# A transformer block on one core: the down projection's operands are split five pairs ahead of their products in place of three

## The chip, the cores and the metric

The kernel runs on one core of one Trainium2 chip. The metric is device time in microseconds (us): lower is better. A core has a matrix engine (TensorE, in the profile PE), a vector engine (VectorE, DVE), a scalar engine (ScalarE, ACT), a general engine (GpSimd, POOL) and a queue that only issues transfers (SyncE, SP). Each engine works through its own list of instructions in order; semaphores tie the lists together.

## The reference, cut to what matters

One decoder layer over 1024 tokens of width 1024, in float32: a mixer (pooling and differential attention, merged and projected), then a SwiGLU feed-forward with a hidden width of 2816, each with an RMSNorm before and after and a residual. The change touches only the last line's product and what follows it:

```python
h = h + rms_norm(einsum('bsd,de->bse', m, w_out), mix_post_g)
u = rms_norm(h, ffn_pre_g)
f = silu(einsum('bsd,df->bsf', u, w_ffn_gate)) * einsum('bsd,df->bsf', u, w_ffn_up)
h = h + rms_norm(einsum('bsf,fd->bsd', f, w_ffn_down), ffn_post_g)
```

## The kernel before, in words

**Precision.** Each float32 operand is split into a high part (a cast to the format that TensorE multiplies, `fp32r`) and a low part (the operand less its high part). A product is three matmuls, high x high, high x low and low x high (`triple`, lines 233 to 235). The cast runs on ScalarE (`split`, line 166), the subtraction on VectorE (`sub`, line 89).

**Seven products.** The down projection f x w_ffn_down is cut in four quadrants and done with seven half-size products in place of eight (a Strassen-like scheme). Each product takes one combination S of the hidden activations, kept in DRAM (`fsd`), and one combination T of the weights, summed in place in SBUF (`wsum`, line 149). The hidden width of a half is 1408, 11 slices of 128; so there are 7 x 11 = 77 pairs (product, slice kb). For one pair `operands` (lines 1180 to 1184) makes two tiles, `s_op` and `w_op`, each with a high and a low part of 128 x 512; TensorE then runs four row tiles x three matmuls, 12 in all. `down_block` accumulates them in the PSUM banks Y, X or Z (`Yd`, `Xd`, `Zd` in the profile).

**Buffers.** `s_op`, `w_op` and the broadcast gain `g2post` come from one pool, `b4`, of 14 buffers. `g2post` keeps one to the end. The raw activations are loaded two slices at a time (`load_s`, line 1176) into the pool `wraw`, two buffers; a buffer is loaded again only when both of its slices have been cast and subtracted.

**The order.** The loop walks the 77 pairs. At pair n it issues the load for pair n + DEPTH + 3, makes the operands of pair n + DEPTH, and then writes the products of pair n. Outside of two stretches written out by hand (not here) a scheduler decides the order in which each engine gets its instructions; the source order and the free buffers are what it starts from.

**The end.** The last product (A22, T4) goes to Y. Its first six slices (SPLIT = 6, kb 0 to 5) are done pair by pair over four row tiles; slices 6 to 10 are done row tile by row tile, 15 matmuls each, so that a tile's end can be finished while the next is multiplied. Beside the first six slices the kernel finishes output tiles 0 to 3: sum of squares (ScalarE, line 130), mean (VectorE, line 1219, `fms`), multiply by the gain (GpSimd, line 1212, `c`), reciprocal root (GpSimd, line 1221, `frstd`), the scaled residual sum in two halves (VectorE, line 1234, `hr`), and two stores issued from ScalarE's queue (line 1236). Tiles 4 to 7 follow with stores from SyncE's queue; their residual loads (line 1225, `hr`) take the buffers of tiles 0 to 3 and so wait for those tiles' stores.

Of the kernel before, what the change touches and what calls it, by code (L numbers as in the profile page):

```python
# [41 lines left out]
def block_kernel(ctx, tc, x, w_in, pool_mix, pool_scale, w_branch_a, lam_q1, lam_k1, lam_q2,  # L42
# [1194 lines left out]

    g2post = b4([P, D], F32, "g2post")
    nc.sync.dma_start(g2post, ffn_post_g.partition_broadcast(P))
    kept, loaded, DEPTH, SPLIT = {}, {}, 3, 6  # L1240
    PARTS = [(0, HALF), (HALF, D)]
    LAST_PARTS = [(HALF, D), (0, 256), (256, HALF)]
    PRODUCTS = [("A11", "B11"), ("S1", "T1"), ("S2", "T2"), ("S4", "B22"), ("S3", "T3"), ("A12", "B21"), ("A22", "T4")]
# [89 lines left out]
```

## Time and profile before

| what | value |
|---|---|
| median of 3 runs | 1273.1 us (1270.13, 1273.1, 1273.31) |
| span of the profiled execution | 1265.6 us |
| ScalarE, busy | 582.7 us (46%) |
| VectorE, busy | 838.6 us (66%) |
| mean granted TensorE clock | 0.998 |

The profile is one execution; its page lists its span, from the first to the last instruction, and no device time of its own. The runs' times also hold what lies ahead of and behind the span. In the rows of the views, a line gives start and duration in us, engine, source line, operation, output <- inputs; a bracket at its end gives the idle time of the engine just before it and what ended it. A group of rows gives the count and the mean. A row of a wait view reads: engine, line <- what it waited for: us in total, times, longest. "ACTq" and "SPq" are the transfers that ScalarE's and SyncE's queues issue.

### The profile page before, as it was taken

The numbers are of one execution on the slowest core, as the hardware profiler recorded it, in microseconds if no ns is written. First come the engines' busy times: TensorE is split into PE (matmuls) and PEld (weight loads), VectorE is DVE, ScalarE is ACT, GpSimd is POOL, SyncE is SP. The second block draws the span as 40 slices with busy tenths as digits, with TensorE's granted clock in tenths as the row PEclk, the third lists the DMA queues.
The fourth block names the chain that finished last, engine by engine and source line by source line (L and its number), as shares of the span: only waits on it lengthen the run. The fifth ranks groups of instructions, "written<-read, shape, count | busy, mean of one in ns | idle before, by whom it ended". The sixth has DMA issues, their size and how long they took to land.

```text
span 1265.6 us, 15699 instructions
## 1 busy us (share of the span) xinstructions
PE 1246.5 (98%) x5912; PEld 1039.1 (82%) x5912; DVE 838.6 (66%) x1296; ACT 582.7 (46%) x1042; POOL 142.7 (11%) x128
## 2 busy tenths in 40 slices
PE   8999999999999999999999999999999999999997
PEld 7888888888788887888888888888888888888886
DVE  5985784534578888855697655655656547955666
ACT  7553344434477774444553333333333333554542
POOL 4100000000201100000102111011111011000221
PEclk9999999999999999999999999999999999999999
DMA  7354338323797108533314322323322368733236
GB/s 253 114 189 132 135 128 243 115 85 117 259 250 206 34 18 283 169 115 134 117 45 139 125 100 89 103 100 108 125 99 84 125 215 279 238 95 105 87 96 208
DMA packets 135452, 179.15 MB, mean 142 GB/s; under 512 B 7632, under 2 KB 90320, under 8 KB 132944
## 3 DMA queue, kind: packets, MB, share of 16 engines
q1 hardware_dynamic: 124544, 146.56, 37.0%
q10 hardware_dynamic: 10832, 31.59, 6.5%
q8 instruction: 46, 0.75, 0.3%
q14 instruction: 30, 0.25, 0.1%
HBM read 124.39 MB, written 53.74 MB: 141 GB/s over the span
## 4 chain that ended last, share of the span: by engine, by line
PE 89%; DVE 3%; ACT 2%; DMA 2%; issue 2%; POOL 1%; SPq 0%; POOLq 0%; DVEq 0%; ACTq 0%
PE Y L235 10%; PE Y L234 10%; PE Y L233 10%; PE X L235 5%; PE X L234 5%; PE X L233 5%; PE Z L235 3%; PE Z L234 3%; PE Z L233 3%; PE Yd L234 3%; PE Yd L235 3%; PE Yd L233 3%; PE o L792 2%; PE branch L233 2%; PE branch L235 2%; PE branch L234 2%
## 5 line engine op out<-in xcount | busy, mean ns | idle before, releaser
L162 DVE TENSOR_TENSOR p<-Z,p 128x512 f32<-128x512 f32 x35 | 24.2, 691 | 163.3 <-PE Z L235 160.7
L234 PE MATMUL Y<-A_lo,Wh 128*128 128x512 f32 x296 | 115.5, 390 | 0.3 <-DVE A_lo L89 0.3
L233 PE MATMUL Y<-A_hi,Wh 128*128 128x512 f32 x296 | 115.2, 389 | 0.0
L235 PE MATMUL Y<-A_hi,Wl 128*128 128x512 f32 x296 | 115.2, 389 | 0.0
L233 PE MATMUL Y<-S_hi,Wh 128*128 128x512 f32 x280 | 109.2, 390 | 0.0
L233 PE MATMUL X<-S_hi,Wh 128*128 128x512 f32 x280 | 109.2, 390 | 0.0
L235 PE MATMUL Y<-S_hi,Wl 128*128 128x512 f32 x280 | 109.1, 390 | 0.0
L234 PE MATMUL Y<-S_lo,Wh 128*128 128x512 f32 x280 | 109.1, 390 | 0.0
L235 PE MATMUL X<-S_hi,Wl 128*128 128x512 f32 x280 | 108.9, 389 | 0.0
L234 PE MATMUL X<-S_lo,Wh 128*128 128x512 f32 x280 | 108.9, 389 | 0.0
L202 ACT CAST Wh<-wf_t 128x1024 fp32r<-128x1024 f32 x70 | 72.8, 1053 | 72.1 <-PE X L234 30.6
L202 ACT CAST Wh<-w_raw 128x1024 fp32r<-128x1024 f32 x72 | 60.6, 843 | 66.7 <-PE Z L234 40.0
L89 DVE TENSOR_TENSOR w_op<-wd,w_op 128x512 fp32r<-128x512 f32 x77 | 56.1, 729 | 52.8 <-ACT w_op L166 52.6
L89 DVE TENSOR_TENSOR Wl<-wf_t,Wh 128x1024 fp32r<-128x1024 f32 x70 | 86.6, 1245 | 4.8 <-ACT Wh L202 4.8
L166 ACT CAST w_op<-wd 128x512 fp32r<-128x512 f32 x77 | 47.9, 622 | 78.1 <-PE Yd L235 31.4
L89 DVE TENSOR_TENSOR Wl<-w_raw,Wh 128x1024 fp32r<-128x1024 f32 x72 | 70.4, 977 | 14.5 <-ACT Wh L202 14.5
L233 PE MATMUL Yd<-w_op,s_op 128*128 128x512 f32 x176 | 68.7, 390 | 0.6 <-ACT w_op L166 0.6
L234 PE MATMUL Yd<-w_op,s_op 128*128 128x512 f32 x176 | 68.7, 390 | 0.3 <-DVE w_op L89 0.3
L235 PE MATMUL Yd<-w_op,s_op 128*128 128x512 f32 x176 | 68.3, 389 | 0.0
L162 DVE TENSOR_TENSOR wf_t<-w_raw,wf_t 128x512 f32<-128x512 f32 x70 | 65.7, 938 | 1.1
L234 PEld LDWEIGHTS Y<-A_lo,Wh 128*128 128x128 f32 x296 | 55.6, 188 | 12.1 <-DVE A_lo L89 0.7
L233 PEld LDWEIGHTS Y<-A_hi,Wh 128*128 128x128 f32 x296 | 55.6, 188 | 11.6
(269 smaller groups left out, 3058.7 us busy)
## 6 DMA issues: line engine op xcount, KB each, us to landing
s_raw<-fsd SPq DMA_DIRECT2D x35, 512.0 KB, 3.6
w_raw<-in_w_in_dram SPq DMA_DIRECT2D x32, 512.0 KB, 4.3
w_raw<-in_w_ffn_gate_dram SPq DMA_DIRECT2D x22, 512.0 KB, 3.8
w_raw<-in_w_ffn_up_dram SPq DMA_DIRECT2D x22, 512.0 KB, 3.8
fsd<-fss SPq DMA_DIRECT2D x11, 1024.0 KB, 3.9
wd<-in_w_ffn_down_dram SPq DMA_DIRECT2D x44, 256.0 KB, 5.4
fsd<-F SPq DMA_DIRECT2D x33, 256.0 KB, 2.3
qkd<-qk_st ACTq DMA_DIRECT2D x16, 512.0 KB, 3.8
```

The costliest lines, as they stand in the source:

```text
L89: nc.vector.tensor_tensor(out=o, in0=a, in1=f32(hi), op=ALU.subtract)
L162: nc.vector.tensor_tensor(out=o, in0=a, in1=b, op=op)
L166: nc.scalar.copy(hi, a)
L202: nc.scalar.copy(hi, a)
L233: nc.tensor.matmul(o, ah, bh, start=start, stop=False, skip_group_check=goes_on)
L234: nc.tensor.matmul(o, ah, bl, start=False, stop=False, skip_group_check=goes_on)
L235: nc.tensor.matmul(o, al, bh, start=False, stop=stop, skip_group_check=goes_on)
L792: nc.tensor.matmul(o, ats[b // 4][:, j, b % 4 * P:(b % 4 + 1) * P], V[:, b, :, :], start=b == 0 and j == 0, stop=b == qb and j == 1)
```

## The change

One number: the loop keeps the operands of five pairs ahead of the products in place of three. Because the load distance is DEPTH + 3, loads are written eight pairs ahead in place of six. Pools, buffer counts, products and their order in the source stay as they are.

```diff
-    kept, loaded, DEPTH, SPLIT = {}, {}, 3, 6
+    kept, loaded, DEPTH, SPLIT = {}, {}, 5, 6
```

The lines that use it, unchanged:

```python
for n in range(DEPTH + 3):
    fetch(n)
for n in range(DEPTH):
    ready[n] = operands(*PRODUCTS[stream[n][0]], stream[n][1])
for n, (i, kb) in enumerate(stream):
    fetch(n + DEPTH + 3)
    if n + DEPTH < len(stream):
        j, kj = stream[n + DEPTH]
        ready[n + DEPTH] = operands(*PRODUCTS[j], kj)
```

## The prediction

> **What bounds the kernel now.** I read the page first, for the busy engine. It gives one span, of 1265.6 us; the median of the runs shown is 1273.1 us, so 7.5 us lie around the span. I make the sum against the span and carry the same difference over to the median.
>
> ```profile
> span 1265.6 us, 15699 instructions
> PE 1246.5 (98%) x5912; PEld 1039.1 (82%) x5912; DVE 838.6 (66%) x1296; ACT 582.7 (46%) x1042; POOL 142.7 (11%) x128
> ```
>
> TensorE is busy 98% of the span. Converting operands earlier can save only what TensorE loses waiting for operands of the down projection. So the second view is who TensorE waited for, over the whole span; only these two of its rows name the down projection (Yd, fed by w_op):
>
> ```profile
> PE Yd L233 <- ACT w_op L166: 0.6, 1, 0.6
> PE Yd L234 <- DVE w_op L89: 0.3, 1, 0.3
> ```
>
> One wait each, 0.9 us together. The third view, TensorE's instructions in order of time, shows where they are:
>
> ```profile
> 1227.48 0.39 PE L233 MATMUL Yd<-w_op,s_op 128*128 128x512 f32 x1
> ...
> 1243.80 0.39 PE L233 MATMUL Yd<-w_op,s_op 128*128 128x512 f32 x1
> ...
> 1245.84 0.39 PE L233 MATMUL Yd<-w_op,s_op 128*128 128x512 f32 x1
> 1246.23 0.50 PE L234 MATMUL Yd<-w_op,s_op 128*128 128x512 f32 x1
> 1246.56 0.40 PE L235 MATMUL Yd<-w_op,s_op 128*128 128x512 f32 x1
> 1247.58 0.50 PE L233 MATMUL Yd<-w_op,s_op 128*128 128x512 f32 x1 [0.62 <-ACT w_op L166]
> 1248.39 0.50 PE L234 MATMUL Yd<-w_op,s_op 128*128 128x512 f32 x1 [0.31 <-DVE w_op L89]
> ...
> 1248.96 0.39 PE L233 MATMUL Yd<-w_op,s_op 128*128 128x512 f32 x1
> ...
> 1258.96 0.39 PE L235 MATMUL Yd<-w_op,s_op 128*128 128x512 f32 x1
> ```
>
> The last product has pairs 0 to 10 (kb). Pairs 0 to 5 take 72 matmuls from 1227.48 to 1243.80, so a matmul starts every 0.2267 us. From 1243.80 the block's first row tile takes pairs 6 to 10, three matmuls each; 1245.84 is pair 9, 1247.58 is pair 10. From 1245.84 to 1248.96 are six steps, 1.36 us at that pace; they took 3.12. **The whole loss in this product is 1.76 us**, for pair 9's low part and both parts of pair 10. After 1248.96 all is steady.
>
> What made pair 10 late is in the chain that ended last, and in the queues of ScalarE and SyncE:
>
> ```profile
> 1241.31 5.06 DMA s_raw<-fsd
> 1233.76 4.55 ACTq L1236 DMA_DIRECT2D out_dram<-hr  x4
> 1238.35 0.62 ACT L166 CAST s_op<-s_raw 128x512 fp32r<-128x512 f32 x1 [6.68 <-DVE hr L1234]
> 1240.05 1.00 ACTq L1236 DMA_DIRECT2D out_dram<-hr  x2
> 1246.39 0.62 ACT L166 CAST s_op<-s_raw 128x512 fp32r<-128x512 f32 x1 [1.19 <-DMA s_raw<-fsd]
> 1246.92 0.61 ACT L166 CAST w_op<-wd 128x512 fp32r<-128x512 f32 x1
> 1237.50 0.33 SPq L1225 DMA_DIRECT2D hr<-h1d  x1
> 1241.31 0.33 SPq L1176 DMA_DIRECT2D s_raw<-fsd  x1
> ```
>
> ScalarE's cast of pair 7's s (1238.35) stood 6.68 us behind the output stores of row tiles 0 and 1 (four issues, 1233.76), which wait for VectorE's finish of these tiles. VectorE took pair 7's s only at 1240.60, and with that the buffer of s_raw came free: pair 10's load was issued at 1241.31, took 5.06 us, and pair 10 was cast at 1246.39 and 1246.92.
>
> **The change, part by part.** Nothing is added or removed: 77 pairs, the same casts, subtractions, loads and matmuls. The source asks for five pairs of lead in place of three, but in the kernel before buffers already set the lead, not DEPTH:
>
> ```profile
> 1224.96 0.62 ACT L166 CAST w_op<-wd 128x512 fp32r<-128x512 f32 x1 [1.58 <-PE Zd L235]
> ```
>
> This is pair 4 of the last product. Its products begin at 1227.48 + 4 x 12 x 0.2267 = 1238.36, 13.4 us later, and a pair lasts 2.72 us: a lead of 4.9 pairs. The cast waits for TensorE to leave a buffer. The pool has 14 buffers, g2post keeps one, and 13 hold 6.5 pairs whatever DEPTH says. In the built programs the order agrees: TensorE's order is the same throughout; those of ScalarE, VectorE, GpSimd and SyncE, with their waits and buffers, are the same up to the end of the sixth product (row 1227.48). **Six of seven products, and all before them, are the same program: 0 us.** What moves is the last product's second half, where the finish of tiles 0 to 3 shares the engines with the last conversions:
>
> - VectorE before: finish 0, s6, finish 1, w6, finish 2, s7, finish 3, w7, s8 ... After: s6, w6, finish 0, s7, finish 1, w7, finish 2, s8, w8, finish 3, s9, w9, s10, w10.
> - ScalarE: pair 7's s passes ahead of the stores; each tile's two stores now stand before w7, s8, s9 and, the last, before s10 and w10.
> - GpSimd: the third multiply passes ahead of the first rstd; tile 3's rstd waits for a mean that now stands behind w8 on VectorE.
> - SyncE: pair 10's load passes ahead of the residual load of tile 4 (1237.50), which waits for tile 0's store.
>
> The rows for the new chain:
>
> ```profile
> 1228.35 3.07 POOL L1212 TENSOR_TENSOR c<-c,g2post 128x512 f32<-128x512 f32 x2 [23.52 <-ACT junk L130]
> 1231.38 0.55 POOL L1221 TENSOR_TENSOR frstd<-fms,mhalf 128x1 f32<-128x1 f32 x1
> 1231.89 1.28 POOL L1212 TENSOR_TENSOR c<-c,g2post 128x512 f32<-128x512 f32 x1
> 1231.96 2.43 DVE L1234 SCALAR_TENSOR_TENSOR hr<-c,frstd,hr 128x512 f32<-128x512 f32 x2 [1.70 <-POOL frstd L1221]
> 1238.46 0.22 DVE L1219 SCALAR_TENSOR_TENSOR fms<-fss,fms 128x1 f32<-128x1 f32 x2
> 1238.69 1.06 POOL L1221 TENSOR_TENSOR frstd<-fms,mhalf 128x1 f32<-128x1 f32 x2 [1.96 <-DVE fms L1219]
> 1239.27 1.41 DVE L1234 SCALAR_TENSOR_TENSOR hr<-c,frstd,hr 128x512 f32<-128x512 f32 x2 [0.59 <-POOL frstd L1221]
> 1240.60 0.68 DVE L89 TENSOR_TENSOR s_op<-s_raw,s_op 128x512 fp32r<-128x512 f32 x1
> 1241.20 1.41 DVE L1234 SCALAR_TENSOR_TENSOR hr<-c,frstd,hr 128x512 f32<-128x512 f32 x2
> 1247.65 0.68 DVE L89 TENSOR_TENSOR w_op<-wd,w_op 128x512 fp32r<-128x512 f32 x1
> ```
>
> Steps: a finish moves VectorE on by 1.33 (1239.27 to 1240.60), a subtraction by 0.60 (1240.60 to 1241.20). A finish beside a GpSimd multiply took 2.43 (1231.96, with 1231.89), one without it 1.41.
>
> 1. GpSimd: two multiplies end at 1231.4 as before, the third at 1232.7 (1.28), the first rstd at 1233.25 (0.55). Finish 0 starts there and not at 1231.96. Two more rstds (1.06 for two) and the fourth multiply keep GpSimd until 1235.6, so finish 0 costs 2.43: 1235.7.
> 2. s7 to 1236.3. **The load of pair 10 goes out there, 5.0 us earlier than 1241.31**, and lands by 1241.4 if it takes 5.06 again. The load is then no longer the last.
> 3. Finish 1 to 1237.6, w7 to 1238.2, finish 2 to 1239.5, s8 and w8 to 1240.7. ScalarE keeps ahead: two stores are 1.0 (1240.05), and the casts follow by 1239.1 for s8.
> 4. Mean, rstd and hand-over took 0.81 (1238.46 to 1239.27): finish 3 from 1241.5 to 1242.9. s9, w9 to 1244.1; TensorE wants pair 9's low part at 1246.07.
> 5. Tile 3's stores leave ScalarE at 1243.9; s10 and w10 are cast by 1245.0 (wanted at 1246.52), and w10's subtraction ends at 1245.8. TensorE wants it at 1246.75: **0.95 us to spare.** In before it ended at 1248.33.
>
> So the stall goes, 1.76 us. Everything after TensorE's last matmul keeps its distance (1258.96 to 1265.6), if nothing else becomes late. The candidate is tile 7's residual load, which waits for tile 3's stores, issued by 1243.9:
>
> ```profile
> DMA to landing us min/median/max: 3.2/3.8/6.0
> DMA to landing us min/median/max: 2.0/2.4/5.9
> ```
>
> The first row is the residual loads, the second the stores. Even with both maxima it lands at 1243.9 + 5.9 + 6.0 = 1255.8, before TensorE's new end of 1257.6. Nothing is paid there.
>
> The step that the trace does not show is how finishes 1 to 3 fare in their new company. Bounds: 1.41 each (no GpSimd beside them), or 2.43 each. I take 1.41, since in step 3 GpSimd has nothing left but one rstd. The GPSIMD Engine Reference of the Trainium skill (Specifications) says that GpSimd's SBUF interfaces are shared with VectorE and that instructions with two SBUF inputs contend. The 2.43 against 1.41 agrees. By that rule the third multiply, now beside three subtractions, may take 1.54 like the first two (3.07 for two); the spare time would be 0.7 and not 0.95, and the sum the same.
>
> **Sum:** 1265.6 - 1.8 = 1263.8 us of span; 1273.1 - 1.8 = **1271.3 us**. That is 0.14%, under the 0.3% (3.8 us) which a measurement of this kernel can tell from no change: in effect the same time.
>
> **The rivals.**
>
> *Part of the stall stays.* If finishes 1 to 3 are slow in part, or ScalarE comes to its stores late, pair 10 is again last. For it: the spare time is only 0.95 us. Against it: the load, which set the old stall, is 5 us earlier. Each microsecond beyond 0.95 costs one: with two finishes at 2.43, lateness 2.04, stall 1.1, gain 0.7: 1272.4 us.
>
> *Slower: stores ahead of the last casts.* Pair 10's casts now queue on ScalarE behind tile 3's stores, these wait for finish 3, and this for an rstd whose mean stands behind w8. It decides when w10 ends after 1248.5, that is 2.7 us later than in step 5. With 2.43 for three finishes (+3.06) and the largest wait for an rstd, 1.70 in place of 0.8 (+0.9), it ends at 1249.8: a stall of 3.0 in place of 1.76, 1274.4 us. Against it: it takes every upper bound at once.
>
> *Slower by far: the clock drops in a longer stall.*
>
> ```profile
> 1243.80:1249.00 5.20, 4.26 (x17) 2.70 (x16) 3.67 (x6) 2.54 (x5) 0.00 (x0) 1.00 0.92 341
> 1259.40:1265.70 6.30, 0.00 (x0) 0.00 (x0) 2.30 (x5) 0.69 (x2) 0.55 (x1) 0.68 0.43 156
> ```
>
> With the old stall the granted clock stayed at 1.00; in 6.3 us without matmuls it averaged 0.68. Were the last 45 matmuls (1248.96 to 1258.96) run at 0.68, they would take 4.8 us more: about 1279 us with the longer stall. TensorE: Matmul & The Clock Gate, in the Trainium skill (Part 1), puts the drop to half rate after an idle window of about 3.4 us. That would be some 10 us here, an estimate; the row at 1.00 agrees that less idle time does nothing.
>
> *Faster by more: the deeper lead works in all seven products.* It would need waits of TensorE there to remove; there are none but the two rows quoted, and the programs are the same. Its price, had each of the other six products lost the same 0.9 us, is 5.4 us: 1265.9 us.
>
> **How the numbers follow.** Forecast (stall gone, 1271.3): 0.66. Part of it stays (1272.4): 0.20. Slower by the stores (1274.4): 0.09. Clock (1279): 0.02. Faster by more: 0.03. The three runs lie from 2.97 below to 0.21 above their median. So the range starts at 1271.3 - 3.0 = 1268.3 and reaches up to the rival of the stores less a little, 1274.0. Beyond 0.3%, that is under 1269.3 or over 1276.9, lie only the last two cases, and the scatter on the low side adds to the first: faster 0.07, same 0.90, slower 0.03.
>
> **What would show it.** Right: the waits of TensorE have no row for Yd; from 1227.48 to the last matmul the pace is unbroken, some 29.7 us from first start to last in place of 31.5; pair 10's s_raw load is issued near 1236 and ahead of tile 4's hr load; casts of s9 and s10 each follow two stores. Step 1 is right if finish 0 starts about 1.3 us later than before. Wrong: a wait on w_op near pair 10, with tile 3's stores just ahead of its cast; or any difference ahead of the last product that two runs of the kernel before do not show as well.

## The result, and the profile after

The kernel after took 1267.08 us (median of 14 runs, 1265.43 to 1270.29), the kernel before, measured beside it, 1270.69 us (14 runs, 1267.21 to 1273.31). The ratio is 0.9978, with a 95% interval of 0.9968 to 0.9989: by the ratio 2.8 us less, between 1.4 and 4.1 (the medians alone differ by 3.6). The forecast gain of 1.8 us (0.14%) lies in that interval. The forecast time of 1271.3 us and its range from 1268.3 us lie above the measured median.

The page of after, for the lines that answer to those of before:

```profile
span 1264.5 us, 15702 instructions
PE 1246.0 (99%) x5912; PEld 1039.4 (82%) x5912; DVE 839.7 (66%) x1296; ACT 583.2 (46%) x1042; POOL 143.7 (11%) x128
```

The profiled execution took 1266.33 us, so 1.8 us lie around its span. TensorE in order of time, first and last matmul of the last product:

```profile
1228.17 0.39 PE L233 MATMUL Yd<-w_op,s_op 128*128 128x512 f32 x1
...
1257.86 0.39 PE L235 MATMUL Yd<-w_op,s_op 128*128 128x512 f32 x1
```

That is 29.69 us, against 1258.96 - 1227.48 = 31.48 us in before: **1.79 us less**. The 131 steps from one matmul's start to the next are even, 0.227 us on average, and the view of waits has no row for Yd any more. From the last matmul's start to the end of the span both kernels take 6.64 us. The first matmul started 0.69 us later than in before, although the two programs are the same up to there; so the spans differ by only 1.1 us.

SyncE's, ScalarE's, GpSimd's and VectorE's queues beside the last product:

```profile
1238.08 0.33 SPq L1176 DMA_DIRECT2D s_raw<-fsd  x1
1238.51 0.38 SPq L1225 DMA_DIRECT2D hr<-h1d  x1
```

```profile
1244.03 1.00 ACTq L1236 DMA_DIRECT2D out_dram<-hr  x2
1245.08 0.63 ACT L166 CAST s_op<-s_raw 128x512 fp32r<-128x512 f32 x1 [2.21 <-DVE hr L1234]
1245.61 0.62 ACT L166 CAST w_op<-wd 128x512 fp32r<-128x512 f32 x1
```

```profile
1229.04 4.70 POOL L1212 TENSOR_TENSOR c<-c,g2post 128x512 f32<-128x512 f32 x3 [23.52 <-ACT junk L130]
1233.83 2.27 POOL L1221 TENSOR_TENSOR frstd<-fms,mhalf 128x1 f32<-128x1 f32 x3
1236.07 1.44 POOL L1212 TENSOR_TENSOR c<-c,g2post 128x512 f32<-128x512 f32 x1
```

```profile
1229.91 0.98 DVE L89 TENSOR_TENSOR w_op<-wd,w_op 128x512 fp32r<-128x512 f32 x1
1230.81 1.78 DVE L89 TENSOR_TENSOR s_op<-s_raw,s_op 128x512 fp32r<-128x512 f32 x1
1232.51 1.38 DVE L1219 SCALAR_TENSOR_TENSOR fms<-fss,fms 128x1 f32<-128x1 f32 x3
...
1234.94 1.42 DVE L1234 SCALAR_TENSOR_TENSOR hr<-c,frstd,hr 128x512 f32<-128x512 f32 x2 [0.45 <-POOL frstd L1221]
1236.27 1.79 DVE L89 TENSOR_TENSOR s_op<-s_raw,s_op 128x512 fp32r<-128x512 f32 x1
...
1246.39 0.68 DVE L89 TENSOR_TENSOR w_op<-wd,w_op 128x512 fp32r<-128x512 f32 x1
```

Because executions reach the last product at different times, I count from its first matmul. Pair 10's load went out 9.91 us behind it (1238.08 - 1228.17), in before 13.83 us (1241.31 - 1227.48), and now ahead of the first residual load. Pair 10's casts stand right behind tile 3's stores, as the order said. Its low part ended 18.90 us behind the first matmul (1246.39 + 0.68); TensorE wanted it at 19.27 (1246.75 - 1227.48 on the steady pace). It had 0.37 us to spare (19.27 - 18.90).

### The profile page after: what moved, and what is told of

Read it like the earlier page. It is cut to its first block, busy times and chain, and to the rows that moved or that the text cites. A ratio compares the mean times of both kernels' runs of the same rounds, so it can differ in the third digit from the quotient of the medians.

```text
span 1264.5 us, 15702 instructions
## 1 busy us (share of the span) xinstructions
PE 1246.0 (99%) x5912; PEld 1039.4 (82%) x5912; DVE 839.7 (66%) x1296; ACT 583.2 (46%) x1042; POOL 143.7 (11%) x128
## 4 chain that ended last, share of the span: by engine, by line
PE 91%; DVE 3%; ACT 2%; DMA 1%; issue 1%; POOL 1%; SPq 0%; POOLq 0%; DVEq 0%; ACTq 0%
PE Y L235 10%; PE Y L234 10%; PE Y L233 10%; PE X L233 5%; PE X L235 5%; PE X L234 5%; PE Yd L233 3%; PE Yd L234 3%; PE Yd L235 3%; PE Z L233 3%; PE Z L234 3%; PE Z L235 3%; PE o L792 2%; PE branch L233 2%; PE branch L235 2%; PE branch L234 2%
```

## The experiments

Two theories are set against each other. Theory of the load: the last product is as long as pair 10's late load makes it. Rival, theory of the order: the conversions come too late on VectorE and ScalarE, and the load's time does not matter. A second rival: the lead itself pays, in all products. In the table, "load" is the time at which the load that counts for pair 10 is issued, in us behind the first matmul of the last product; the length of the last product runs from the first matmul's start to the last's. Kernels marked "one run" are judged by that length alone.

| kernel | edit | load | last product, us | ratio to before (95%) |
|---|---|---|---|---|
| before | depth 3 | 13.83 | 31.48 | 1 |
| null3 | none | 13.85 | 31.31 | 1.0002 (0.9991 to 1.0012) |
| own3 | load in a buffer of its own | ahead of the product | 30.52 | 0.9999 (0.9989 to 1.0009) |
| depth1 | DEPTH 1 | 17.49 | 36.12 | 1.0045 (1.0032 to 1.0059) |
| depth2 | DEPTH 2 | 15.14 | 32.31 | one run |
| depth4 | DEPTH 4 | 11.77 | 29.69 | one run |
| after | DEPTH 5 | 9.91 | 29.69 | 0.9978 (0.9968 to 0.9989) |
| late5 | program of after | 9.91 | 29.69 | 0.9991 (0.9980 to 1.0002) |
| depth7 | DEPTH 7 | 8.15 | 29.69 | 0.9995 (0.9983 to 1.0006) |
| twice5 | DEPTH 5, load made twice | 12.94 | 30.51 | 0.9996 (0.9987 to 1.0006) |
| thrice5 | DEPTH 5, load made three times | 17.84 | 36.90 | 1.0051 (1.0035 to 1.0067) |
| sp3 | depth 3, stores on SyncE | 14.05 | 30.36 | one run |
| nomul5 | DEPTH 5, without GpSimd's multiply of c11 | 6.54 | 29.69 | one run |

**null3**: the kernel before against itself, no edit.

> The kernel before, unchanged, measured against itself. It shows how far two measurements of one program differ, and whether the stall at the end of the last product is there in every execution. By both theories: ratio 1.000 within 0.001, last product 31.5 us from the first matmul's start to the last's (31.48 in before, 29.69 in after).

Measured: ratio 1.0002, 31.31 us. The same two waits are there, a little shorter than in before:

```profile
PE Yd L233 <- ACT w_op L166: 0.4, 1, 0.4
PE Yd L234 <- DVE w_op L89: 0.3, 1, 0.3
```

So the stall belongs to the kernel, not to one execution, and two sets of runs of one program differ by about 0.1% either way. A change of 0.14% is at the edge of what the times can show; the length of the last product shows it plainly.

**own3**: pair 10's load moved, the order kept.

```diff
-        t = wp.tile([P, 2, HALF], F32, tag="wraw", bufs=2, name=name("s_raw"))
+        if S == "A22" and n == 1:
+            t = sm.tile([P, 1, HALF], F32, tag="last", bufs=1, name=name("s_raw"))
+        else:
+            t = wp.tile([P, 2, HALF], F32, tag="wraw", bufs=2, name=name("s_raw"))
```

> Depth 3 as before, but the raw activations of pair 10 of the last product are loaded into a buffer of their own, so that the load waits for no conversion; the order on VectorE, ScalarE and GpSimd stays that of before. If the late load is the cause (theory of the load): the wait for the transfer goes, pair 10 is cast at about 1245.6 and its low part ends at about 1247.4 in before's times; 0.7 to 1.0 us of the 1.79 come back, last product 30.5 to 30.8 us. If the order of the conversions is the cause (rival): the load moves and nothing else, last product 31.3 to 31.5 us.

Measured: 30.52 us. TensorE's waits in the last product:

```profile
PE Yd L234 <- DVE w_op L89: 0.2, 1, 0.2
```

Of the 1.79 us (1.62 from null3) about 0.8 to 1.0 come back. The wait for ScalarE's cast is gone, one for VectorE's low part stays. (The view counts only the time in which TensorE does nothing; by the matmuls' starts 0.83 us are lost here, as 1.79 us are in before, where the view has 0.9.) What holds pair 10 now, in own3's rows (its lines 1237 and 89 are the finish and the subtraction):

```profile
1245.45 0.62 ACT L166 CAST s_op<-s_raw 128x512 fp32r<-128x512 f32 x1 [1.32 <-DVE hr L1237]
```

```profile
1246.11 0.69 DVE L89 TENSOR_TENSOR s_op<-s_raw,s_op 128x512 fp32r<-128x512 f32 x1 [0.47 <-ACT s_op L166]
...
1249.12 0.69 DVE L89 TENSOR_TENSOR w_op<-wd,w_op 128x512 fp32r<-128x512 f32 x1
```

ScalarE's cast of pair 8's s stands behind the stores of finish 3, and VectorE's last six subtractions follow it without a pause. The last ends 19.91 us behind the product's start (1229.90), 0.64 us after TensorE wants it (19.27). In after only four subtractions stand behind finish 3. **Neither theory alone is right**: the load is worth about half of the stall, the place of the conversions behind finishes on VectorE and ScalarE the other 0.83 us (30.52 - 29.69).

**late5** was to hold back pair 10's load in after's order.

```diff
+        if S == "A22" and n == 1:
+            wp.tile([P, 2, HALF], F32, tag="wraw", bufs=2, name=name("skip"))
```

> Depth 5 as after, with after's order on every engine, but pair 10's load gets the other buffer and has to wait for pair 9's subtraction (at 1244.6 in after) in place of pair 7's. Theory of the load: issued near 1245.2, lands 3.5 to 5 us later, pair 10 stalls TensorE by 3.0 to 5.0 us; last product 32.7 to 34.7 us, 0.2 to 0.4% slower than after. Rival (order of the conversions): the order is after's, so last product about 30 us. The stall is also long enough to see whether the granted clock falls.

Measured: 29.69 us, load at 9.91 us. The tile that nothing writes did not move the load; every engine's order and the load's time are those of after, so this tests neither theory and is a second measurement of after: 0.9991, beside 0.9978. Both fit the 0.14%.

**twice5** and **thrice5** hold the load back with after's order unchanged on TensorE, VectorE, ScalarE and GpSimd (thrice5: range(2)):

```diff
+        for _ in range(1 if S == "A22" and n == 1 else 0):
+            t = wp.tile([P, 2, HALF], F32, tag="wraw", bufs=2, name=name("s_raw"))
+            nc.sync.dma_start(t[:, :n], fsd[kb:kb + n, :, FSLOT[S], :].rearrange("k p c -> p k c"))
```

> Depth 5 with after's order on every engine, but the raw activations of pair 10 are loaded twice into the same buffer, so that the valid load waits for the first to land and for a residual load ahead of it on SyncE (a transfer of 256 KB more). In after's times the second goes out near 1241.5, lands at 1245.5 to 1246.6, and pair 10's cast, at 1245.1 in after, comes 0.5 to 1.5 us later. Theory of the load: last product 29.8 to 31.0 us in place of 29.69. Theory of the order alone: 29.7 us, as after.

> As twice5 with a third load of the same data, behind one more residual load: out near 1246.5 in after's times, landed at 1250 to 1251. Theory of the load: TensorE idles some 4 us before pair 10, and if an idle time like that of depth1 (3.98 us) halves the matmul pace for some 8 matmuls again, 1.6 us more: last product 34.5 to 37 us. Theory of the order alone: 29.7 us.

Measured: twice5 30.51 us, thrice5 36.90 us, both in their ranges. The load that counts, in the chain that ended last:

```profile
1240.74 4.99 DMA s_raw<-fsd
```

```profile
1250.40 4.63 DMA s_raw<-fsd
```

The first row is twice5's, the second thrice5's. The order is after's, and the later load brings a stall back: 0.82 us more than after at 12.94, 7.21 us more at 17.84. Of the 7.21 us some 1.9 are slower matmuls behind the idle time (nine steps from 1257.06 to 1261.04 took 3.98 us in place of 2.04). The theory of the order alone falls. With after's order the load costs nothing at 9.91 and counts at 12.94, where it takes 4.99 us to land; where between them it begins to count was not tried.

**depth1, depth2, depth4, depth7**: one number changed in `kept, loaded, DEPTH, SPLIT = {}, {}, 3, 6`.

> One pair ahead in place of three. The built order differs from before's only in the last product: three finishes or more pass ahead of pair 7's conversion, and three residual loads stand ahead of pair 10's load. Theory of the load: load near 1243.5 in before's times, low part of pair 10 near 1250.4, stall 3 to 4 us; last product 33 to 34 us, and the first six products without a wait. If DEPTH did set the lead in all products: waits on w_op in each of the seven, the total some 5 us or more over before.

> Two pairs ahead: on VectorE pair 7's activations come behind all four finishes, and pair 10's load stands behind two residual loads on SyncE. Theory of the load: load some 2 to 4 us later against the product's start than in before (13.8 us), last product 32.5 to 35.5 us, between depth 3 (31.4) and depth 1 (36.1). If the lead paid smoothly, pair by pair, depth 2 would lie halfway between them, at 33.8 us, and depth 4 halfway between depth 3 and 5, at 30.6 us.

> Four pairs ahead: pair 7's activations come behind two finishes, pair 10's load ahead of every residual load. Theory of the load: load 1 to 2 us later against the product's start than in after (9.9 us), still landed in time; last product 29.7 us, at most 30.0.

> Seven pairs ahead, more than the 13 free buffers hold; the built order lets the last conversions pass further ahead of finishes, and TensorE's order is the same. Theory of the load, and theory of the order too: with no wait left in after there is nothing to gain; last product 29.7 us, ratio to after 1.000, ratio to before 0.998 to 0.999. If the lead itself paid, it would be faster than after by as much again as after is than before.

Measured: 36.12, 32.31, 29.69 and 29.69 us. depth2 lay 0.2 us under its range, depth1 2.1 us over. depth2's load went out 1.3 us later than before's (15.14 and 13.83), where 2 to 4 were expected. The six other products had no wait on operands in any of the four: the only row in which TensorE waits for ScalarE's w_op was, for depth1 and then depth2,

```profile
PE Yd L233 <- ACT w_op L166: 4.0, 1, 4.0
```

```profile
PE Yd L233 <- ACT w_op L166: 1.5, 1, 1.5
```

It is not a smooth curve in the lead: depth 2 lies near depth 3 and not halfway to depth 1, depth 4 at the floor and not halfway. From DEPTH 4 down to 1 the product gets longer as pair 10's load goes out later; order and load move together here, so these runs alone do not separate the two theories. The rival "the lead pays in all products" falls: even with DEPTH 1 and 2 the traces have before's order on every engine up to the last product, and no wait there. DEPTH 4 already has all there is, and depth7 gains nothing more (its ratio, 0.9995, came out above the expected 0.998 to 0.999; the interval reaches down to 0.9983). depth1 is longer than expected because its load went out 17.49 us behind the product's start and not at about 16.0 (1243.5 - 1227.48), and because the clock fell, below.

**sp3**: stores of tiles 0 to 3 moved off ScalarE's queue, at depth 3.

```diff
-            finish(kb - 1, residual(kb - 1), PARTS, [nc.scalar.dma_start])
+            finish(kb - 1, residual(kb - 1), PARTS, [nc.sync.dma_start])
```

> Depth 3 with the stores of tiles 0 to 3 issued from SyncE in place of ScalarE. ScalarE's casts then wait for no store, but pair 10's load stands behind three tiles' stores and a residual load on SyncE. Theory of the load: it is issued no earlier than in before (13.8 us behind the product's start), last product 31 to 32.5 us. If ScalarE's stores ahead of the casts were the cause: 29.7 to 30.3 us.

Measured: 30.36 us, between the two ranges. The load went out as late as in before, but it landed faster, and the cast followed at once. ScalarE's row and VectorE's last ones:

```profile
1247.92 0.62 ACT L166 CAST s_op<-s_raw 128x512 fp32r<-128x512 f32 x1 [5.57 <-DMA s_raw<-fsd]
```

```profile
1247.29 0.69 DVE L89 TENSOR_TENSOR w_op<-wd,w_op 128x512 fp32r<-128x512 f32 x1
...
1249.10 0.68 DVE L89 TENSOR_TENSOR s_op<-s_raw,s_op 128x512 fp32r<-128x512 f32 x1
1249.70 0.68 DVE L89 TENSOR_TENSOR w_op<-wd,w_op 128x512 fp32r<-128x512 f32 x1
```

The chain that ended last gives the load 3.19 us (1244.70 to 1247.89), in before 5.06. My lower bound took the 5 us for granted; with it pair 10 would have been cast 1.9 us later. The edit also changed more than the queue of the stores: with ScalarE's casts free, pair 7's and pair 8's s pass ahead of finishes 2 and 3 on VectorE. What is left of the stall, 0.67 us (30.36 - 29.69), is VectorE's: five subtractions without a pause behind finish 3, of which pair 10's s begins 0.56 us after its cast has ended (1248.54). So the stores in ScalarE's queue are not the whole of the second half of the stall. What made the load slow in before is not settled.

**nomul5**: GpSimd's multiply of c11 by the gain left out.

```diff
-                half_done(tb, 0, c11[:, tb], c11[:, tb], nc.gpsimd)
+                half_done(tb, 0, c11[:, tb], c11[:, tb], None)
```

(With None, `half_done` leaves the multiply out; that line of the edit is not shown.)

> Depth 5 without GpSimd's multiply of the first halves of tiles 0 to 3 by the gain: those outputs lack the gain of their first 512 columns. It asks what made three of VectorE's instructions long in after (0.98, 1.78 and 1.79 us in place of 0.68). If they stretch because GpSimd multiplies beside them: all subtractions at 0.68 to 0.7 us, pair 10's low part ready 1 to 2 us earlier against TensorE's first matmul of the last product (18.9 us behind it in after); last product 29.7 us, no change, since nothing waited. If GpSimd is not the cause: the long ones stay.

Measured: 29.69 us. Two of VectorE's three long subtractions of after (0.98 and 1.78 us there), the three means behind them (1.38 us there), and pair 10's low part:

```profile
1230.39 0.68 DVE L89 TENSOR_TENSOR w_op<-wd,w_op 128x512 fp32r<-128x512 f32 x1
1231.12 0.69 DVE L89 TENSOR_TENSOR s_op<-s_raw,s_op 128x512 fp32r<-128x512 f32 x1
1231.73 0.29 DVE L1220 SCALAR_TENSOR_TENSOR fms<-fss,fms 128x1 f32<-128x1 f32 x3
...
1243.50 0.68 DVE L89 TENSOR_TENSOR w_op<-wd,w_op 128x512 fp32r<-128x512 f32 x1
```

All subtractions are back at 0.68 to 0.69 us, and pair 10's low part ends 15.53 us behind the product's start (1243.50 + 0.68 - 1228.65), 3.4 us earlier than in after, where 1 to 2 were forecast. GpSimd's multiply stretched the instructions beside it: after's four long rows (0.98, 1.78, 1.38 and 1.79) are together 3.6 us longer than the same work here (0.68, 0.69, 0.29 and 0.68). The product's length does not move, since TensorE waits for nothing in either.

## Why the prediction was right and wrong, point by point

**The change: right.** The programs are the same for six products; a 1.76 us stall was forecast to go and 1.79 went; the end kept its distance. "Some 29.7 us from first start to last" is what was measured. The 0.3% taken as the least that a measurement can tell was too coarse: null3's interval is 0.1% either way, and that of after does not hold 1.

**The base: wrong, and with it the time and the range.** The step that failed is "the median of the runs shown is 1273.1 us, so 7.5 us lie around the span. I make the sum against the span and carry the same difference over to the median". Around a span lie 1.8 us, as after's profiled execution shows (1266.33 and 1264.5); in every run on record whose span is known it is 1.7 to 1.9. The profiled execution of before, with a span of 1265.6 us, thus took about 1267.4 us (1265.6 + 1.8, an estimate), close to the lowest of the 14 times (1267.21), and was none of the three on which the forecast stood. The other 5.7 us (1273.1 - 1267.4) were the difference between executions: the profile came from a short one, while two of the three times, 1273.1 and 1273.31, turned out to be the highest of 14. The range took its scatter from these three. With the base of the 14 runs, 1270.69, the same sum gives 1268.9 us. Of the miss of 4.2 us (1271.3 - 1267.08) the base makes 2.4. The other 1.8 us nothing in the last product accounts for, and the next set of runs did not repeat them: late5, the same program, gave 1268.04 beside 1269.25 for before, 1.2 us apart.

**The chain that leads to 0.95 us of spare time: right in the end, by errors that offset each other in part.** Spare time was 0.37 us. The forecast had pair 10's load 8.80 us behind the product's start (1236.28 - 1227.48) and it went out at 9.91. Step 1 put finish 0 at 1233.25; measured on before's times it started at 1234.25 (1234.94 - 0.69). The three multiplies took 4.70 us together, and the subtraction, the means and the rstds beside them 1.78, 1.38 and 2.27 us. Finish 0 then took 1.42 and not 2.43: GpSimd was at its rstds, and the fourth multiply (1236.07) came only at its end. s7, which began 0.20 us behind that multiply, took the stretch in its place (1.79). Step 5 let both of tile 3's stores wait for the end of finish 3 (1242.9 and 1.0 for two); in after they begin before that end (1244.03, with finish 3 ending at 1244.67), which gave some 0.5 us back. In the prediction the stretch fell on the finishes and the multiplies alone; nomul5 shows that the subtractions pay too. The rule of the GPSIMD Engine Reference in the Trainium skill (Specifications), that VectorE's instructions with two SBUF inputs contend with GpSimd, covers them, and nomul5 agrees (0.68 and 0.69 us without the multiplies).

**The cause: half right.** I named the late load as what made pair 10 late. own3 shows that the load is worth about half; the other half is the conversions' place behind the finishes. That the sum did not suffer is luck: the change moves both, and the forecast reckoned with the stall as a whole.

**The rivals.** Part of the stall staying, and slower by stores ahead of casts: neither came, though 0.37 us was near. The clock: right as a mechanism, wrong in size. It fell only where the load was held back (depth1, thrice5), and not for the rest of the product:

```profile
1252.06 0.50 PE L233 MATMUL Yd<-w_op,s_op 128*128 128x512 f32 x1 [3.98 <-ACT w_op L166]
1252.87 0.80 PE L234 MATMUL Yd<-w_op,s_op 128*128 128x512 f32 x1 [0.31 <-DVE w_op L89]
1253.46 0.63 PE L235 MATMUL Yd<-w_op,s_op 128*128 128x512 f32 x1
1253.89 0.63 PE L233 MATMUL Yd<-w_op,s_op 128*128 128x512 f32 x1
...
1256.02 0.50 PE L235 MATMUL Yd<-w_op,s_op 128*128 128x512 f32 x1
1256.36 0.39 PE L233 MATMUL Yd<-w_op,s_op 128*128 128x512 f32 x1
```

In depth1, after 3.98 us without work, matmuls start every 0.43 us until 1256.0 and every 0.23 from 1256.36 on: under 2 us lost, where I had 4.8 for 45 matmuls. TensorE: Matmul & The Clock Gate, in the Trainium skill (Part 1), gives both the half rate after an idle window and the return after a busy window of about 3.4 us; the row agrees with the return (1252.9 to 1256.4; in thrice5 1257.1 to 1261.0), and I had used only the fall. The fall itself came here behind shorter waits too (2.34 us in depth7, last section).

**A version faster than both** did not turn up: depth4, after and depth7 have no wait left in the last product.

## What to carry to other kernels

A number in the source that asks for more lead does nothing where free buffers already set the lead; compare the built order of the two kernels first, and only the stretch that differs needs a sum. There, look for what stands ahead of the last load in every queue, and do not stop at the first late thing found: with the load moved, about half of the stall was still there. Before an absolute time is forecast from one profiled execution, ask whether that execution was a typical one, and compare its span with the times it is to be joined to; the difference of two times was right here, while the base was off by 2.4 us.

## What the runs showed of the hardware that was not expected

Executions of one program differ ahead of the change: the first matmul of the last product started at 1227.48 us in before, at 1229.68 in null3, the same program, and at 1232.56 in thrice5, whose program is the same up to there. Part of it shows in the granted clock of two stretches, here in before and then in thrice5; the column ahead of the last two is the clock:

```profile
320.00:340.00 20.00, 18.15 (x80) 14.48 (x78) 8.78 (x11) 10.67 (x14) 7.67 (x4) 1.00 0.75 246
480.00:500.00 20.00, 17.85 (x99) 14.41 (x98) 16.56 (x39) 7.46 (x27) 2.01 (x2) 1.00 1.03 359
```

```profile
320.00:340.00 20.00, 16.32 (x66) 13.10 (x65) 7.47 (x8) 8.35 (x12) 7.66 (x4) 0.91 0.74 221
480.00:500.00 20.00, 17.15 (x100) 14.69 (x98) 14.72 (x37) 9.07 (x34) 2.02 (x2) 0.91 0.85 297
```

In the first stretch TensorE waits once for a transfer, 1.9 us in before and 3.7 in thrice5:

```profile
PE s L751 <- DMA QB<-qkd: 1.9, 1, 1.9
```

```profile
PE s L751 <- DMA QB<-qkd: 3.7, 1, 3.7
```

Over 13 profiled executions the clock of that stretch was 1.00 in the four whose wait was 1.7 to 2.1 us, and 0.91 in eight of the nine whose wait was 2.3 to 3.7 us (1.00 in nomul5, with 2.6). In order of time the fall follows the wait: in depth7 TensorE waited 2.34 us, up to 334.72, and its matmuls start every 0.43 us from 336.05 to 339.03 and every 0.23 from 339.36 on. That the wait triggers the fall was not tried by an experiment of its own. If it does, a few tenths of a microsecond in a transfer can cost more than their own length later.

GpSimd's multiplies stretched subtractions on VectorE by a factor of 2.6 (1.78 in after against 0.69 in nomul5). Yet one in before took its usual time beside them. VectorE's row, and then GpSimd's first two multiplies one by one (the prediction has them as a group, 3.07 us for two):

```profile
1229.59 0.68 DVE L89 TENSOR_TENSOR w_op<-wd,w_op 128x512 fp32r<-128x512 f32 x1
```

```profile
1228.35 1.29 POOL L1212 TENSOR_TENSOR c<-c,g2post 128x512 f32<-128x512 f32 x1 [23.52 <-ACT junk L130]
```

```profile
1229.60 1.82 POOL L1212 TENSOR_TENSOR c<-c,g2post 128x512 f32<-128x512 f32 x1
```

Here the subtraction started 0.01 us ahead of the second multiply, and the multiply paid. The one that starts second pays, in every case that the traces hold: in the 12 executions with these multiplies, one overlaps a finish's half or a subtraction of VectorE by 0.1 us or more 57 times. VectorE's instruction, where it started second (32 times), ended 0.55 us behind the multiply's end; the multiply, where it started second (25 times), ended 1.14 to 1.16 us behind VectorE's. So the second seems to do most of its work (0.68 and 1.29 us alone) only after the first has ended. A mean over a group hides this: the prediction read 1.54 us for each of the two multiplies that took 1.29 and 1.82.
